# Attention scores of two heads on the two halves of TensorE's rows, in a two-layer decoder trunk

## The chip, the cores and the metric

The kernel runs on one core of a Trainium2 chip. The metric is the device time of one execution in microseconds (us), smaller is better. Three runs of the kernel before took 1722.72, 1716.74 and 1719.22 us: a median of 1719.22 us.

Engines are named as the profile names them: PE is TensorE's matmuls and PEld its weight loads, DVE is VectorE, ACT is ScalarE, POOL is GpSimd, SP is SyncE, whose queue issues the DMAs (its rows read SPq). "L381" is line 381 of the kernel.

## What is computed

Two layers over 1024 tokens of width 1024. The first mixes tokens with dilated sliding-window attention (three groups, 16 heads of 64), the second with grouped-query sliding-window attention (16 query heads over 2 key heads, with a learned sink logit per head). After each comes an output projection, a layer norm and a gated per-layer embedding. Cut to what matters here:

```python
def apply_rope(t, cos, sin):
    t1, t2 = t[..., :32], t[..., 32:]
    return concatenate([t1 * c - t2 * s, t2 * c + t1 * s], -1)

def banded_attention(q, k, v, max_dist, sinks=None):   # blocks of 128 queries
    s = einsum('bnqhgd,bnkhd->bnhgqk', qb, kw) * 64 ** -0.5
    s = where(mask, s, -inf)
    m = max(s, -1)                    # with sinks: m = maximum(m, sk)
    e = exp(s - m)
    l = sum(e, -1)                    # with sinks: l = l + exp(sk - m)
    return einsum('bnhgqk,bnkhd->bnqhgd', e, vw) / l, m + log(l)
```

## The kernel before

**Numbers.** Every factor of a product is split into two f16 parts, high and low, and three of the four products of parts are summed: high by high, high by low, low by high. A projection (`lin`, L262) so takes 24 matmuls of 128x512 for one tile of 128 tokens by 512 columns.

**Layer A** (`layer_a`, L620) goes twice over three groups. In each it takes a block of V weights and two blocks of Q and K weights; each block is multiplied with 8 tiles of tokens. **Layer B** (`layer_b`, L782) takes one block for keys and values, two for queries, two for the gate. Weight blocks come in by DMA, DVE takes their maximum (L108, four instructions a block), and ACT and DVE split them (L131, L132, four each), all in steps between the tiles.

**Rotation.** `rope_out` (L333) multiplies a projected tile in PSUM with cosine and sine on DVE (L344, twice), then POOL takes a difference for the first halves of the heads and a sum for the second (L346, L347). ACT rounds to the high part (L353) and POOL subtracts it (L354). One head's high and low parts, 64 columns each, lie side by side. For keys DVE copies them a second time with high and low exchanged (L357). One DMA transposes all blocks of 128 columns (L358): 4 queries, 4 keys and 4 exchanged keys in layer A. The transposed block of a head holds the high part on partitions 0 to 63 and the low one on 64 to 127, so a matmul over all 128 rows against the keys, and a second one against the exchanged keys, give the sum of all four products.

**Units.** The attention of 128 queries and four heads against one or two blocks of 128 keys is a unit; there are 96 in layer A and 32 in layer B. `scores` (L368) makes two PSUM tiles `s`, one for each pair of heads, fills each with its matmuls (L381), and has DVE add the mask and take the row maxima (L385, one instruction for each head and a short one that reads the maximum out). DVE then turns maxima into biases (L387; in layer B also L389, a minimum with the sinks), ACT takes the four exponentials (L391) and the f16 high part (L395), POOL or DVE the low part (L397), and a DMA transposes both to `pT` (L400). `pv` (L403) multiplies `pT` with the values, 12 matmuls of 64 columns for a block of keys (L412 to L414).

**Order.** `unit_step` (L298) takes up the scores of a new unit and the `pv` of the one taken up two units before (layer A) or three (layer B). Tiles come from pools of rotating buffers, and waits are put in where a buffer is written after a read. The program is then reordered for each engine by a list scheduler with a timeline of its own, so the order on an engine is not that of the code. Each engine runs its own instructions strictly in that order.

**Tables.** Cosines, sines, masks and the identity lie in one tile `tab`, loaded once at the start (L452, L458).

Of the kernel before, what the change touches and what calls it, by code (L numbers as in the profile page):

```python
# [20 lines left out]
P = 128  # L21
S = 1024
D = 1024
# [30 lines left out]
def const_table():  # L54
# [5 lines left out]
    for o in token_orders():  # L60
        for t in (cos, sin):
            rope.append(t[o].transpose(1, 0, 2).reshape(P, NT * 32))
# [22 lines left out]
N_ROPE = 6 * NT * 32  # L85
N_CONST = N_ROPE + 6 * P

# [51 lines left out]
class Trunk:  # L139
    def __init__(self, ctx, tc, a):  # L140
# [30 lines left out]
        self.cos, self.sin = [], []  # L171
        for o in range(3):
            for i, lst in enumerate((self.cos, self.sin)):
                b = (2 * o + i) * NT * 32
                lst.append(tab[:, b:b + NT * 32].rearrange("p (n c) -> p n c", n=NT))
        b = N_ROPE
# [13 lines left out]
    def keep(self, cols=1, name="k"):  # L190
        self.uid += 1
        return self.const.tile([P, cols], F32, name=f"{name}{self.uid}", tag=f"{name}{self.uid}")

# [139 lines left out]
    def rope_out(self, ps, nq, nk, order, n, dst):  # L333

        nc, w = self.nc, self.work
        nh = nq + nk
        t1 = w.tile([P, 512], F32, tag="t1", name="t1")
        t2 = w.tile([P, 512], F32, tag="t2", name="t2")  # L340
        pv = ps.rearrange("p (h c) -> p h c", c=32)
        for t, tb in ((t1, self.cos[order]), (t2, self.sin[order])):
            tv = t[:, :nh * HD].rearrange("p (h c) -> p h c", c=32)
            nc.vector.tensor_mul(tv, pv, tb[:, n, :].unsqueeze(1).to_broadcast([P, 2 * nh, 32]))  # L344
        v1, v2 = (t[:, :nh * HD].rearrange("p (h b c) -> p h b c", b=2, c=32) for t in (t1, t2))
        nc.gpsimd.tensor_sub(v1[:, :, 0, :], v1[:, :, 0, :], v2[:, :, 1, :])  # L346
        nc.gpsimd.tensor_add(v1[:, :, 1, :], v1[:, :, 1, :], v2[:, :, 0, :])  # L347
        nb = nh + nk
        hl = w.tile([P, 12, P], F16, tag="hl", name="hl", bufs=3)
        rv = t1[:, :nh * HD].rearrange("p (h c) -> p h c", c=HD)  # L350
# [17 lines left out]
    def scores(self, qa, kas, mask, cs, ncs, sums, nbias, floor, pool_lo):  # L368
# [65 lines left out]
    def startup(self):  # L434
# [4 lines left out]
        with tc.tile_pool(name="start", bufs=1) as st:  # L439
# [12 lines left out]
            nc.sync.dma_start(self.tab[:, N_CONST - P:], a["tab"][:, N_CONST - P:])  # L452
# [5 lines left out]
            nc.sync.dma_start(self.tab[:, :N_CONST - P], a["tab"][:, :N_CONST - P])  # L458
# [161 lines left out]
    def layer_a(self):  # L620
# [14 lines left out]
        for pair in range(2):  # L635
            for g in (1, 2, 0):
                blk = self.next_block()
# [9 lines left out]
                for i in range(2):  # L647
# [4 lines left out]
                    for n in range(NT):  # L652
                        ps = self.ps_lin.tile([P, 512], F32, tag="lin", name="lin")
                        self.lin(ps, blk, *self.stat_a(g, n), 0, 512)
                        qk.append(at.tile([P, 12, P], F16, tag="qk", name="qk", bufs=8))
                        self.rope_out(ps, 4, 4, g, n, qk[n])
# [22 lines left out]
    def unit_a(self, q, g, n, qk, vh, vl, cs, ncs, cv, scr):  # L679
# [22 lines left out]
        kas = [lambda h, sw, t=qk[i]: t[:, 4 + 4 * sw + h, :] for i in tiles]  # L702
        self.later(UNIT_LAG, lambda: self.unit(lambda h: qk[n][:, h, :], kas, mask, cs, ncs,
# [78 lines left out]
    def layer_b(self, xT, invx):  # L782
# [5 lines left out]
        self.nsink = self.kv.tile([P, 16], F32, name="nsink", tag="nsink")  # L788
        nc.vector.tensor_scalar(self.nsink, self.sinks, -1.0, LN_PSCALE, op0=ALU.mult, op1=ALU.add)
# [3 lines left out]
        kT = [self.kv.tile([P, 4, P], F16, tag=f"bk{n}", name="bk") for n in range(NT)]  # L793
        vh = self.kv.tile([P, NT, 2, HD], F16, tag="bvh", name="bvh")
        vl = self.kv.tile([P, NT, 2, HD], F16, tag="bvl", name="bvl")
        for n in range(NT):
# [3 lines left out]
            self.rope_out(ps[:, :P], 0, 2, 0, n, kT[n])  # L800
# [3 lines left out]
        for kv in range(2):  # L804
# [5 lines left out]
            nc.vector.tensor_scalar(ncs, cs, -1.0, None, op0=ALU.mult)  # L810
            for n in range(NT):
# [3 lines left out]
                self.rope_out(ps, 8, 0, 0, n, qT)  # L815
# [8 lines left out]
    def unit_b(self, kv, n, hg, qT, kT, vh, vl, cs, ncs, cv, tile_st):  # L824
        nc, at, sp = self.nc, self.att, self.small
        tiles = [n] if n == 0 else [n - 1, n]
        kas = [lambda h, sw, t=kT[i]: t[:, 2 * sw + kv, :] for i in tiles]
# [25 lines left out]
        self.later(UNIT_LAG, lambda: self.unit(lambda h: qT[:, 4 * hg + h, :], kas, mask, cs, ncs,  # L853
# [281 lines left out]
```

## Time and profile before

| | |
|---|---|
| median of 3 runs | 1719.22 us |
| the profiled execution, its own time | 1715.05 us |
| its span, first to last instruction | 1713.3 us |
| PE busy | 1595.0 us (93%) |
| DVE busy | 1163.1 us (68%) |
| ACT busy | 837.6 us (49%) |
| POOL busy | 700.2 us (41%) |
| mean granted clock of TensorE | 0.98 |

The busy time of PE counts a matmul from its start to its modelled end, and matmuls overlap; how much of PE a matmul really takes is read from the distance of one start to the next. Idle time before an instruction is put down to what ended it. The rows in question stand two sections below.

### The profile page before, as it was taken

The page shows a single profiled execution, that of the slowest core. Times are in us where ns is not written, and L with a number is a line of the kernel's source. Part 1 is how long each engine was busy: PE and PEld are TensorE (multiplying, and loading weights), DVE is VectorE, ACT ScalarE, POOL GpSimd, SP SyncE. Part 2 cuts the span into 40 slices and gives each one's busy share as a digit, 9 for nine tenths or more (in the row PEclk, how much of TensorE's full clock was granted, in tenths as well). Part 3 has the DMA queues.
Part 4 walks back from the last instruction along what each step waited for, and adds up shares of the span by engine and source line. Part 5 has one row for each costly group of instructions (what it writes and reads, how often), then busy time and mean ns, then how long its engine had stood idle before and what let it go on. Part 6 is the DMA issues. An engine that isn't in the chain of part 4 may idle for free. (4 is left out here: it accounts for less than half of the span.)

```text
span 1713.3 us, 29175 instructions
## 1 busy us (share of the span) xinstructions
PE 1595.0 (93%) x10579; PEld 882.3 (51%) x10579; DVE 1163.1 (68%) x2846; ACT 837.6 (49%) x1818; POOL 700.2 (41%) x601
## 2 busy tenths in 40 slices
PE   9899999999998889999999988689999898979998
PEld 3455566654555456666545543234464555534444
DVE  6767656765677776567567776787457988767731
ACT  4425554554654365545545663523334677753221
POOL 1115524532655665155235553443324553123431
PEclk9999999999999999999999999799999999989999
DMA  9618865764778787477558887989965798787963
GB/s 367 225 59 163 161 142 128 161 142 117 154 155 220 184 165 153 112 155 162 120 131 169 182 221 224 297 226 259 251 172 113 143 188 179 170 277 217 239 201 111
DMA packets 542785, 309.06 MB, mean 180 GB/s; under 512 B 473008, under 2 KB 494128, under 8 KB 542256
## 3 DMA queue, kind: packets, MB, share of 16 engines
q1 hardware_dynamic: 542640, 307.20, 73.2%
q8 instruction: 83, 1.36, 0.3%
q14 instruction: 62, 0.51, 0.1%
HBM read 135.82 MB, written 54.92 MB: 111 GB/s over the span
## 5 line engine op out<-in xcount | busy, mean ns | idle before, releaser
L268 PE MATMUL lin<-whl,xhl 128*128 128x512 f16 x1280 | 488.1, 381 | 0.0
L269 PE MATMUL lin<-whl,xhl 128*128 128x512 f16 x1280 | 486.9, 380 | 0.0
L270 PE MATMUL lin<-whl,xhl 128*128 128x512 f16 x1280 | 486.5, 380 | 0.0
L391 ACT ACTIVATE sm<-sm,st,cs 128x128 f32<-128x128 f32 (+1 forms) x384 | 203.6, 531 | 171.1 <-DVE st L387 144.2
L397 POOL TENSOR_TENSOR phl<-sm,phl 128x1024 f16<-128x1024 f32 (+1 forms) x88 | 160.3, 1821 | 257.2 <-ACT phl L395 240.5
L108 DVE TENSOR_REDUCE wpm<-wraw 128x1 f32<-128x1024 f32 (+1 forms) x132 | 156.8, 1197 | 93.2 <-DMA wraw<-in_wa_dram 49.8
L270 PEld LDWEIGHTS <-xhl 128*128 128x128 f16 x1280 | 149.0, 116 | 126.8 <-issue 1.9
L268 PEld LDWEIGHTS <-xhl 128*128 128x128 f16 x1280 | 149.0, 116 | 118.2 <-issue 1.8
L269 PEld LDWEIGHTS <-xhl 128*128 128x128 f16 x1280 | 149.8, 117 | 115.6 <-issue 1.3
L346 POOL TENSOR_TENSOR t<-t,t 128x256 f32<-128x256 f32 (+1 forms) x120 | 93.4, 778 | 275.1 <-DVE t L344 265.3
L354 POOL TENSOR_TENSOR hl<-t,hl 128x512 f16<-128x512 f32 (+1 forms) x120 | 140.2, 1169 | 102.5 <-ACT hl L353 102.5
L385 DVE CUSTOM_DVE_ANT_0 sm<-s,tab 128x256 f32<-128x256 f32 (+1 forms) x512 | 157.2, 358 | 30.8 <-PE s L381 26.5
L344 DVE TENSOR_TENSOR t<-lin,tab 128x512 f32<-128x512 f32 (+1 forms) x240 | 147.6, 654 | 28.0 <-PE lin L270 27.8
L132 DVE SCALAR_TENSOR_TENSOR whl<-wraw,s,whl 128x1024 f16<-128x1024 f32 (+1 forms) x116 | 156.6, 1394 | 3.1 <-ACT whl L131 3.1
L353 ACT ACTIVATE hl<-t 128x512 f16<-128x512 f32 (+1 forms) x120 | 72.3, 603 | 174.8 <-POOL t L347 155.7
L131 ACT ACTIVATE whl<-wraw,s 128x1024 f16<-128x1024 f32 (+1 forms) x116 | 122.0, 1123 | 21.7 <-DVE s L208 14.0
L268 PE MATMUL lin<-whl,x2T 128*128 128x512 f16 (+1 forms) x320 | 116.5, 364 | 0.0
L270 PE MATMUL lin<-whl,x2T 128*128 128x512 f16 (+1 forms) x320 | 116.2, 363 | 0.0
L269 PE MATMUL lin<-whl,x2T 128*128 128x512 f16 (+1 forms) x320 | 116.2, 363 | 0.0
L395 ACT ACTIVATE phl<-sm 128x1024 f16<-128x1024 f32 (+1 forms) x128 | 110.7, 865 | 2.2
L412 PEld LDWEIGHTS <-pT 128*128 128x128 f16 x800 | 72.4, 98 | 51.6 <-DMA pT<-phl 49.3
L357 DVE COPY hl<-hl 128x512 f16<-128x512 f16 (+1 forms) x104 | 50.4, 484 | 71.5 <-POOL hl L354 71.2
(189 smaller groups left out, 2940.1 us busy)
## 6 DMA issues: line engine op xcount, KB each, us to landing
wraw<-in_wa_dram SPq DMA_DIRECT2D x56, 512.0 KB, 5.5
scr<-st SPq DMA_DIRECT2D x96, 132.0 KB, 2.5
gt<-scr SPq DMA_DIRECT2D x48, 264.0 KB, 3.4
wraw<-in_wav_dram SPq DMA_DIRECT2D x24, 512.0 KB, 5.8
prh<-pro SPq DMA_DIRECT2D x32, 256.0 KB, 3.6
wraw<-in_wg_dram SPq DMA_DIRECT2D x16, 512.0 KB, 7.0
wraw<-in_wb_dram SPq DMA_DIRECT2D x16, 512.0 KB, 5.6
xg<-y SPq DMA_DIRECT2D x16, 512.0 KB, 3.8
```

Source lines behind the costliest of these rows:

```text
L108: k.nc.vector.tensor_reduce(pm[:, c:c + 1], self.raw[:, c * q:(c + 1) * q], axis=AX.X, op=ALU.max, apply_absolute_value=True)
L131: nc.scalar.activation(hl[:, 0, sl], self.raw[:, sl], AF.Copy, scale=self.s)
L132: nc.vector.scalar_tensor_tensor(hl[:, 1, sl], self.raw[:, sl], self.s, hl[:, 0, sl], op0=ALU.mult, op1=ALU.subtract)
L268: mm(ps, xh(kt), wh, start=(kt == 0), stop=False)
L269: mm(ps, xh(kt), wl, start=False, stop=False)
L270: mm(ps, xl(kt), wh, start=False, stop=(kt == NK - 1))
L344: nc.vector.tensor_mul(tv, pv, tb[:, n, :].unsqueeze(1).to_broadcast([P, 2 * nh, 32]))
L354: nc.gpsimd.tensor_sub(hl[:, :nh, HD:P], rv, hl[:, :nh, 0:HD])
L385: nc.vector.tensor_tensor_reduce(sm[:, h, :nk], ps[:, i, :nk], mask, 1.0, -3e38, ALU.add, ALU.max, mx[:, h:h + 1])
L391: nc.scalar.activation(sm[:, h, :nk], sm[:, h, :nk], AF.Exp, bias=nbias[:, h:h + 1], scale=cs, accum_out=sums[:, h:h + 1])
L395: nc.scalar.activation(hl[:, 0], sm[:, :, :nk], AF.Copy)
L397: eng.tensor_sub(hl[:, 1], sm[:, :, :nk], hl[:, 0])
```

## The change

**Scores.** High and low parts are no longer side by side for each head: all high parts come first, then all low parts. A transposed block of 128 columns then holds one part of two heads, head 0 of the pair on partitions 0 to 63 and head 1 on 64 to 127. A score matmul now reads 64 rows, the upper or the lower half (the program gives it a tile of 64x128 at row 0 or at row 64), and there are three for each head and block of keys: high by high, high by low, low by high. The copy of exchanged keys goes away, and the transposing DMAs have 8 blocks instead of 12 in layer A, 2 instead of 4 for the keys of layer B. The two PSUM tiles of a unit now belong to the two halves, and each holds the scores of that half's head for both pairs. In layer B the heads are reordered in the weights so that the two heads of a pair use different key heads.

**Biases.** DVE no longer computes the biases; one ACT instruction does. With sinks, DVE takes a maximum with scaled sinks ahead of it.

**Rotation.** The sine table holds minus sine and sine; DVE's second product reads the heads' halves exchanged, and POOL makes one sum of 512 columns instead of a difference and a sum of 256. The tables of a group are loaded when the group starts, 384 KB each, seven times in all, into two buffers.

```diff
-    def rope_out(self, ps, nq, nk, order, n, dst):
+    def rope_out(self, ps, nq, nk, n, dst):
...
-        for t, tb in ((t1, self.cos[order]), (t2, self.sin[order])):
-            tv = t[:, :nh * HD].rearrange("p (h c) -> p h c", c=32)
-            nc.vector.tensor_mul(tv, pv, tb[:, n, :].unsqueeze(1).to_broadcast([P, 2 * nh, 32]))
-        v1, v2 = (t[:, :nh * HD].rearrange("p (h b c) -> p h b c", b=2, c=32) for t in (t1, t2))
-        nc.gpsimd.tensor_sub(v1[:, :, 0, :], v1[:, :, 0, :], v2[:, :, 1, :])
-        nc.gpsimd.tensor_add(v1[:, :, 1, :], v1[:, :, 1, :], v2[:, :, 0, :])
+        cos = self.cos[:, n, :].unsqueeze(1).to_broadcast([P, 2 * nh, 32])
+        nc.vector.tensor_mul(t1[:, :nh * HD].rearrange("p (h c) -> p h c", c=32), pv, cos)
+        pb = ps.rearrange("p (h b c) -> p h b c", b=2, c=32)[:, :, ::-1, :]
+        sin = self.sin[:, n].unsqueeze(1).to_broadcast([P, nh, 2, 32])
+        nc.vector.tensor_mul(t2[:, :nh * HD].rearrange("p (h b c) -> p h b c", b=2, c=32), pb, sin)
+        nc.gpsimd.tensor_add(t1[:, :nh * HD], t1[:, :nh * HD], t2[:, :nh * HD])
...
-            nc.scalar.activation(hl[:, :nh, 0:HD], rv, AF.Copy)
-            nc.gpsimd.tensor_sub(hl[:, :nh, HD:P], rv, hl[:, :nh, 0:HD])
-            if nk:
-                src, to = (hl[:, a:b, :].rearrange("p h (w c) -> p h w c", w=2) for a, b in ((nq, nh), (nh, nb)))
-                nc.vector.tensor_copy(to, src[:, :, ::-1, :])
-            nc.sync.dma_start(dst, hl[:, :nb, :].rearrange("p b c -> p (b c)"), transpose=True)
+            nc.scalar.activation(hl[:, :m], t1[:, :m], AF.Copy)
+            nc.gpsimd.tensor_sub(hl[:, m:2 * m], t1[:, :m], hl[:, :m])
+            nc.sync.dma_start(dst, hl[:, :2 * m], transpose=True)
...
+        ps = [self.ps_s.tile([P, 2, 2 * P], F32, tag="s", name="s") for _ in range(2)]
         for pr in range(2):
-            ps = self.ps_s.tile([P, 2, 2 * P], F32, tag="s", name="s")
+            for kb, ka in enumerate(kas):
+                for j, (x, y) in enumerate(((0, 0), (0, 1), (1, 0))):
+                    for i in range(2):
+                        rows = slice(HD * i, HD * i + HD)
+                        nc.tensor.matmul(ps[i][:, pr, kb * P:(kb + 1) * P], qa(pr, x)[rows], ka(pr, y)[rows],
+                                         start=(j == 0), stop=(j == 2))
             for i in range(2):
                 h = 2 * pr + i
-                for kb, ka in enumerate(kas):
-                    for sw in range(2):
-                        nc.tensor.matmul(ps[:, i, kb * P:(kb + 1) * P], qa(h), ka(h, sw), start=(sw == 0),
-                                         stop=(sw == 1))
-            for i in range(2):
-                h = 2 * pr + i
-                nc.vector.tensor_tensor_reduce(sm[:, h, :nk], ps[:, i, :nk], mask, 1.0, -3e38, ALU.add, ALU.max,
+                nc.vector.tensor_tensor_reduce(sm[:, h, :nk], ps[i][:, pr, :nk], mask, 1.0, -3e38, ALU.add, ALU.max,
                                                mx[:, h:h + 1])
-        nc.vector.tensor_scalar(nbias, mx, ncs, LN_PSCALE, op0=ALU.mult, op1=ALU.add)
         if floor is not None:
-            nc.vector.tensor_tensor(nbias, nbias, floor, op=ALU.min)
+            nc.vector.tensor_max(mx, mx, floor)
+        nc.scalar.activation(nbias, mx, AF.Copy, scale=ncs, bias=LN_PSCALE)
```

**What the order becomes on PE.** The scheduler's order changes with it. In the kernel before, TensorE meets the second pair of a unit's heads right behind the first, in another PSUM tile. These rows are that place in a unit of layer A with two blocks of keys (`qk` holds transposed queries and keys; a DVE wait here is for a reader of an earlier unit):

```order
L381 LDWEIGHTS qk
L381 MATMUL s<-qk 128x128
L381 LDWEIGHTS qk [waits DVE_49]
L381 MATMUL s<-qk 128x128 [waits PE_49]
```

In the changed kernel the second pair goes into the same two PSUM tiles as the first, and its first matmul into each of them waits for DVE. These rows of PE are a second pair in layer A; its first pair stands 10 projection matmuls and 14 value matmuls ahead:

```order
L411 MATMUL o<-vl,pT 128x64
L379 LDWEIGHTS qk
L379 MATMUL s<-qk 128x128 [waits DVE_49]
L379 LDWEIGHTS qk
L379 MATMUL s<-qk 128x128
L379 LDWEIGHTS qk
L379 MATMUL s<-qk 128x128 [waits DVE_49]
...
L379 MATMUL s<-qk 128x128
L412 LDWEIGHTS pT
L412 MATMUL o<-vh,pT 128x64
```

The second pair has moved away from the first, here into the middle of another unit's value matmuls. Over the program the 1600 score matmuls of before stand in 149 uninterrupted stretches, the 2400 of the changed kernel in 259. Within these, 406 of the 2400 follow a matmul on the same half of the rows; taken in pairs of different halves where they alternate, they make 983 pairs and 434 single ones. In every unit the program's wait of the second pair names the reductions of the first; the projection and value matmuls in between are worth 1.2 to 7.6 us at the distances of [Rows 3] below, with a median of about 4.

**And on DVE.** Before, these rows of DVE are one unit of layer A (L385, four maxima), then its biases (L387), the copy of exchanged keys (L357) and the next tile's rotation (L344):

```order
L385 ISA sm,mx<-s,tab 128x256 [waits PE_49]
L385 ISA mx 128x1
L385 ISA sm,mx<-s,tab 128x256
L385 ISA mx 128x1
L385 ISA sm,mx<-s,tab 128x256 [waits PE_49]
L385 ISA mx 128x1
L385 ISA sm,mx<-s,tab 128x256
L385 ISA mx 128x1
L387 TENSOR_SCALAR st<-mx,ncs_4250 128x4 [waits DMAHW5_49,DVE_49]
L357 COPY hl<-hl 128x512 [waits DMAHW1_49,Pool_49]
L344 TENSOR_TENSOR t_4713<-lin,tab 128x512 [waits PE_49]
```

In the changed kernel the two pairs of a unit stand apart, here with a tile's rotation between them:

```order
L383 ISA sm,mx<-s,tab 128x256 [waits PE_49]
L383 ISA mx 128x1
L383 ISA sm,mx<-s,tab 128x256 [waits PE_49]
L383 ISA mx 128x1
L345 TENSOR_TENSOR t_4625<-lin,rope 128x512 [waits PE_49,Pool_49]
L348 TENSOR_TENSOR t_4626<-lin,rope 128x512
L383 ISA sm,mx<-s,tab 128x256 [waits DVE_49,PE_49]
L383 ISA mx 128x1
```

The biases and the copy are gone, and the rotation has moved between the first pair's maxima and the second's.

## Rows read from the trace of the kernel before

**Rows 1.** The page: span, then busy time, share and instructions of each engine.

```profile
span 1713.3 us, 29175 instructions
PE 1595.0 (93%) x10579; PEld 882.3 (51%) x10579; DVE 1163.1 (68%) x2846; ACT 837.6 (49%) x1818; POOL 700.2 (41%) x601
```

**Rows 2.** Windows of 100 us: busy us (instructions) of PE to POOL, PEclk, DMA share, GB/s.

```profile
500.00:600.00 100.00, 88.06 (x633) 50.37 (x632) 78.16 (x191) 45.79 (x109) 59.27 (x47) 0.95 0.77 192
700.00:800.00 100.00, 98.35 (x657) 67.88 (x656) 63.16 (x174) 51.92 (x133) 41.43 (x44) 1.00 0.66 138
1300.00:1400.00 100.00, 89.11 (x832) 51.72 (x830) 92.21 (x270) 64.91 (x172) 52.15 (x45) 0.97 0.76 153
```

**Rows 3.** Timeline of PE in layer A: start and length in us, instruction, count.

```profile
306.97 0.61 PE L381 MATMUL s<-qk 128*128 128x128 f16 x8
307.42 0.19 PE L412 MATMUL o<-vh,pT 128*128 128x64 f16 x1
307.45 0.19 PE L413 MATMUL o<-vl,pT 128*128 128x64 f16 x1
...
308.02 0.38 PE L269 MATMUL lin<-whl,xhl 128*128 128x512 f16 x1
...
314.71 0.38 PE L270 MATMUL lin<-whl,xhl 128*128 128x512 f16 x1
```

**Rows 4.** Groups by line and shape: busy us, mean ns of one, idle before.

```profile
L381 PE MATMUL s<-qk 128*128 128x128 f16 x1120 | 79.0, 220 | 5.4 <-DMA qk<-hl 5.3
L381 PEld LDWEIGHTS <-qk 128*128 128x128 f16 x1120 | 70.6, 98 | 26.8 <-DMA qk<-hl 7.2
L381 PE MATMUL s<-bk,bq 128*128 128x128 f16 x480 | 35.8, 221 | 2.1 <-DMA bq<-hl 2.1
```

**Rows 5.** Waits of PE alone: total us, times, longest us.

```profile
PE o L412 <- DMA pT<-phl: 39.8, 31, 4.0
PE s L381 <- DMA qk<-hl: 5.3, 2, 4.7
```

**Rows 6.** Waits of all engines, same columns.

```profile
DVE hl L357 <- POOL hl L354: 71.2, 42, 3.6
DVE sm L385 <- PE s L381: 26.5, 22, 2.8
```

**Rows 7.** Timeline of one unit of layer A, the last column what it waited for.

```profile
503.03 1.06 PE L381 MATMUL s<-qk 128*128 128x128 f16 x16
504.44 0.41 DVE L385 CUSTOM_DVE_ANT_0 sm<-s,tab 128x256 f32<-128x256 f32 x1
505.47 0.42 DVE L385 CUSTOM_DVE_ANT_0 sm<-s,tab 128x256 f32<-128x256 f32 x1
507.39 3.85 DVE L132 SCALAR_TENSOR_TENSOR whl<-wraw,s,whl 128x1024 f16<-128x1024 f32 x2
511.17 0.22 DVE L387 TENSOR_SCALAR st<-mx,ncs 128x4 f32<-128x4 f32 x1
511.42 0.60 ACT L391 ACTIVATE sm<-sm,st,cs 128x256 f32<-128x256 f32 x1 [2.57 <-DVE st L387]
```

**Rows 8.** Groups by line and shape on DVE, POOL and ACT, columns as in rows 4.

```profile
L385 DVE CUSTOM_DVE_ANT_0 sm<-s,tab 128x256 f32<-128x256 f32 x288 | 106.0, 416 | 19.3 <-PE s L381 15.0 <-POOL phl L397 4.3
L385 DVE DVE_READ_ACCUMULATOR2_ANT mx<- 128x1 f32 x512 | 41.3, 81 | 0.0
L387 DVE TENSOR_SCALAR st<-mx,ncs 128x4 f32<-128x4 f32 x96 | 40.9, 426 | 1.6
L387 DVE TENSOR_SCALAR sb<-mx,ncs 128x4 f32<-128x4 f32 x32 | 15.7, 493 | 0.3
L357 DVE COPY hl<-hl 128x512 f16<-128x512 f16 x96 | 48.6, 507 | 67.9 <-POOL hl L354 67.7
L132 DVE SCALAR_TENSOR_TENSOR whl<-wraw,s,whl 128x1024 f16<-128x1024 f32 x112 | 152.3, 1403 | 2.7 <-ACT whl L131 2.7
L346 POOL TENSOR_TENSOR t<-t,t 128x256 f32<-128x256 f32 x112 | 89.8, 802 | 266.6 <-DVE t L344 258.4 <-DVE se L842 3.3 <-DVE mde L224 3.0
L758 POOL TENSOR_TENSOR gt<-gt 128x512 f32<-128x512 f32 x16 | 22.7, 1419 | 1.0
L746 ACT ACTIVATE mw<-mw 128x24 f32<-128x24 f32 x16 | 3.5, 219 | 53.9 <-DVE mw L745 53.9
```

**Rows 9.** DMA issues: size or count, median us from issue to landing.

```profile
pT<-phl SPq DMA_TRANSPOSE x128, 4.4
qk<-hl SPq DMA_TRANSPOSE x96, 4.0
```

More of the change, by code (lines that the diff above doesn't have):

```diff
@@ L60, in const_table @@
     for o in token_orders():
-        for t in (cos, sin):
-            rope.append(t[o].transpose(1, 0, 2).reshape(P, NT * 32))
+        for t in (cos, np.concatenate([-sin, sin], 1)):
+            rope.append(t[o].transpose(1, 0, 2).reshape(P, -1))
     r = np.arange(P)[:, None]
@@ L170, in __init__ @@
         self.tab = tab
[L171 to L176, printed above, removed]
+        b = 0
         self.mask_a = tab[:, b:b + 2 * P]
@@ L192, in keep, with rope_tables @@
         return self.const.tile([P, cols], F32, name=f"{name}{self.uid}", tag=f"{name}{self.uid}")
+    def rope_tables(self, order):
+        t = self.const.tile([P, N_ROPE], F32, name="rope", tag="rope", bufs=2)
+        self.nc.sync.dma_start(t, self.a["tab"][:, order * N_ROPE:(order + 1) * N_ROPE])
+        self.cos = t[:, :NT * 32].rearrange("p (n c) -> p n c", n=NT)
+        self.sin = t[:, NT * 32:].rearrange("p (n b c) -> p n b c", n=NT, b=2)
     def pow2(self, mx, s, inv):
@@ L700, in outp @@
                 self.merges.append(self.merge(n, q // 2, scr[q // 2]))
-        kas = [lambda h, sw, t=qk[i]: t[:, 4 + 4 * sw + h, :] for i in tiles]
-        self.later(UNIT_LAG, lambda: self.unit(lambda h: qk[n][:, h, :], kas, mask, cs, ncs,
+        kas = [lambda j, x, t=qk[i]: t[:, 4 * x + 2 + j, :] for i in tiles]
+        self.later(UNIT_LAG, lambda: self.unit(lambda j, x: qk[n][:, 4 * x + j, :], kas, mask, cs, ncs,
                                           lambda h, kb: vh[:, tiles[kb], h, :], lambda h, kb: vl[:, tiles[kb], h, :],
@@ L787, in layer_b @@
         self.bufs = 3
-        self.nsink = self.kv.tile([P, 16], F32, name="nsink", tag="nsink")
-        nc.vector.tensor_scalar(self.nsink, self.sinks, -1.0, LN_PSCALE, op0=ALU.mult, op1=ALU.add)
+        self.rope_tables(0)
+        self.sk_cs = self.kv.tile([P, 16], F32, name="sk_cs", tag="sk_cs")
         blk = self.next_block()
@@ L792, in layer_b @@
         ck = self.prod(invx, blk.inv, 2.0 ** QK_SHIFT, "ck")
-        kT = [self.kv.tile([P, 4, P], F16, tag=f"bk{n}", name="bk") for n in range(NT)]
+        kT = [self.kv.tile([P, 2, P], F16, tag=f"bk{n}", name="bk") for n in range(NT)]
         vh = self.kv.tile([P, NT, 2, HD], F16, tag="bvh", name="bvh")
@@ L826, in unit_b @@
         tiles = [n] if n == 0 else [n - 1, n]
-        kas = [lambda h, sw, t=kT[i]: t[:, 2 * sw + kv, :] for i in tiles]
+        kas = [lambda j, x, t=kT[i]: t[:, x, :] for i in tiles]
         mask = self.mask_b[:, (2 - len(tiles)) * P:]
@@ L851, in outp @@
             nc.sync.dma_start(self.o_dr[n][:, c0 * HD:(c0 + 4) * HD], u)
-        self.later(UNIT_LAG, lambda: self.unit(lambda h: qT[:, 4 * hg + h, :], kas, mask, cs, ncs,
-                                          lambda h, kb: vh[:, tiles[kb], kv, :], lambda h, kb: vl[:, tiles[kb], kv, :],
-                                          stats, outp, hg == 1, self.nsink[:, c0:c0 + 4], after if hg else None))
+        self.later(UNIT_LAG, lambda: self.unit(lambda j, x: qT[:, 4 * x + 2 * hg + j, :], kas, mask, cs, ncs,
+                                          lambda h, kb: vh[:, tiles[kb], h % 2, :], lambda h, kb: vl[:, tiles[kb], h % 2, :],
+                                          stats, outp, hg == 1, self.sk_cs[:, c0:c0 + 4], after if hg else None))
     def transpose_rows(self, src, s, dst, i, name):
@@ L1106, in _layout, with heads @@
     a["ao"] = halves(f["a_w_out"][0])
-    a["bo"] = halves(f["b_w_out"][0])
+    turn = np.arange(16).reshape(2, 8).T.ravel()
+    def heads(m):
+        return m.reshape(m.shape[0], 16, HD)[:, turn].reshape(m.shape[0], 1024)
+    a["bo"] = halves(f["b_w_out"][0].reshape(16, HD, D)[turn].reshape(D, D))
     a["wg"] = np.stack([halves(f["ple_w_gate"][l]) for l in range(2)])
```

30 lines of the change are left out of this document (17 added, 13 removed).

## The prediction, made before the changed kernel ran

> **What bounds the kernel now.** I read the page's busy times first. PE is busy for 1595.0 of 1713.3 us, the next engine, DVE, for 1163.1 [rows 1]. Then the windows, because a mean hides stages: in 700 to 800 PE is busy for 98.35 us of 100, so there only PE's own work counts; in 500 to 600 it is 88.06 and in 1300 to 1400 89.11 with DVE at 92.21 [rows 2], so there something else sets the pace part of the time. What it is stands in the waits of PE: 39.8 us in 31 cases in front of a unit's first value matmul, for the transposed probabilities `pT` [rows 5]. There are 96 + 32 = 128 units (the counts of L387 in [rows 8]), so about 31 of 128 units, 24%, go at the pace of the chain from scores to `pT`, and the other 76% at the pace of PE.
>
> What one matmul takes of PE is the distance of starts. Eight score matmuls start at 306.97 and the next instruction at 307.42: 56 ns each. Two value matmuls are 29 ns apart (307.42, 307.45), projection matmuls 216 ns (31 steps from 308.02 to 314.71) [rows 3]. Each of them has a weight load of its own, and that load's record is 98 ns long [rows 4], so at these distances the loads run behind other matmuls.
>
> **The change part by part.**
>
> *Score matmuls.* Before: 1120 + 480 = 1600 [rows 4] by 56 ns = 89.6 us. After: 2400 of the same 128 columns. If two on different halves run at the same time, a pair takes the longer of one matmul (56 ns) and two issues with their loads (2 x 29 = 58 ns, the pace of the value matmuls). The order leaves 983 such pairs and 434 single ones: 983 x 58 + 434 x 56 ns = 81.3 us, **8.3 us less**. No row shows overlap. Bounds: all 1200 as pairs, 69.6 us (20 less); none overlapping, 2400 x 56 ns = 134.4 us (44.8 more). I take the overlap, since operands, rows and PSUM tiles of the two are separate.
>
> *Change of the tile's shape.* All matmuls of before use 128 rows, so no row shows TensorE going from 128 to 64 rows and back. The changed order does it 2 x 259 = 518 times. If it is free, 0. If the array has to be empty first, the matmul in front is waited for to its end: 0.38 - 0.216 us for a projection (its record's length less the step, [rows 3]) and 220 - 56 ns for a score [rows 3, 4], both 165 ns: 518 x 165 ns = 85 us. If the first load can't hide either, 98 ns more each: 136 us. I take half of the 165 ns, 82 ns, since a recorded end is modelled and holds more than the way through the array: **42.7 us**. [...]
>
> *A new wait inside each unit.* The second pair's matmuls now wait for the first pair's maxima on DVE. What is queued behind them on PE is everything: value and projection matmuls. DVE needs two maxima of 416 + 81 ns [rows 8], 1.0 us, once it gets to them, and it seldom does at once: it was found idle and waiting for scores only 22 times [rows 6] in 256 pairs. In the unit of [rows 7] the maxima start 1.4 us after the scores, and a run of weight splits that follows holds DVE for 3.85 us. The order covers the wait with 1.2 to 7.6 us of other matmuls, about 4 at the median. A run of four splits is 4 x 1.403 = 5.6 us [rows 8], 1.6 beyond the cover; some 24 blocks are split in the attention stages, 24 x 1.6 = 38 us if each run met a waiting pair. I take a third, **12 us**. Bounds: 0, and 38.
>
> *The chain to `pT`.* The second pair's scores come about 4 us later than before. Shorter by: two maxima, since the first pair's are done by then, 1.0 us; the biases' step on DVE, 0.43 us (L387), taken over by ACT at about 0.22 (L746) with the same four exponentials behind it; the copy L357, 0.51 us, and DVE's wait for POOL ahead of it, 71.2 us over 104 copies, 0.68 each [rows 6, 8]. 4.0 - 1.0 - 0.43 + 0.22 - 0.51 - 0.68 = 1.6 us longer. A unit's values come two units after its scores, so in the 31 units that wait, each costs half of it, 0.8 us: 25 us. In [rows 7] the biases stood behind 5.4 us of other DVE work after the last maximum began, which the change takes out of the chain there, so I take **18**. Bounds: 0, and 31 x 1.5 = 46 (the 3 us without any relief).
>
> *Relief of DVE in layer B.* L387 leaves: 15.7 us [rows 8]. In 1300 to 1400 DVE and PE are about equally close to full [rows 2], so half counts: **8 us less**. Bounds: 0 and 15.7. Layer A's share (40.9 + 48.6 us) is hidden under PE, other than in the chain above.
>
> *No cost:* POOL's one sum, at most 1419 (L758) instead of twice 802 ns (L346) [rows 8], with POOL 41% busy. The transposes of `qk` with a third fewer blocks: they land in 4.0 us [rows 9], and PE waited for them 5.3 us in all [rows 5]; that is what it would give at most. Seven loads of tables on SP's queue: each is issued as its group starts and first read a V block later, 8 x 24 x 216 ns = 41 us of cover; without that cover one would cost some 4 us.
>
> *Sum.* PE's own work: -8.3 + 42.7 + 12 = 46.4 us, of which 76% reach the end: 35. With 18 and -8: +45. The profiled execution took 1715.05 us, so 1760; the median of the runs is 4.2 us above it, so **1764 us**.
>
> **Rivals.**
>
> *Faster: TensorE changes shape for nothing.* Then 518 x 82 ns go, and if DVE, with 40.9 + 15.7 + 48.6 us less to do and 71.2 us less to wait, keeps ahead of the second pairs, so do the 12. -8.3 x 0.76 = -6; half of the chain's 18, +9; relief 15.7: together -13, **1706 us**. For it: at 56, 29 and 216 ns TensorE passes from one kind of matmul to another without a gap [rows 3]. Against it: these all have the same shape. It decides below 33 ns a change: with the other terms as here, (-8.3 + 518 x 0.033) x 0.76 + 9 - 15.7 = 0.
>
> *Slower: the change of shape costs the whole way out.* 165 ns: (-8.3 + 85 + 12) x 0.76 + 10 = +77, **1797 us**; with the load in the open, 1835. For it: the two differences in the rows agree at 165 ns. [...]
>
> *The change doesn't do what it says: halves run one after another.* Then +44.8 in place of -8.3: (44.8 + 42.7 + 12) x 0.76 + 10 = +86, **1805 us**; with a free change of shape +53, 1772. For it: a matmul of 64 rows has as many columns as one of 128, and no row shows two at once. [...]
>
> **How the numbers follow.** Forecast (1764): 0.44. Free change of shape (1706): 0.26. Full price (1797 to 1835): 0.17. No overlap (1772 to 1805): 0.13. The range has to leave out no more than 0.2: from 1700, below the faster case with its chain bound at 0, to 1820, past no overlap and the nearer half of the full price. Within 0.3% is 1714 to 1724 us, about what a measurement of this kernel can tell from no change. The faster case lies under it 3 times in 4 (0.195), the forecast's own low end now and then (0.015): faster 0.21. Same 0.07, from the upper end of the faster case and the lower end of the forecast. Slower 0.72.
>
> **What would show it.** In the profile of the changed kernel: starts of score matmuls in twos a few ns apart, pairs some 58 ns apart, show the overlap; 56 ns throughout refute it. The distance from the last projection matmul to the first score matmul, and from the last score to the next projection matmul, beyond 216 and 56 ns, is the price of a change of shape: about 80 ns each by the forecast, nothing or 165 by the rivals. Waits of PE's scores on L383, near 12 us or more, show the new wait; hardly any refute it. Waits for `pT` above 39.8 us show the longer chain, below it that the relief weighs more. The forecast is wrong if the changes of shape are free and PE's waits fall: then the time is under 1714.

## The result, and the profile after

The changed kernel takes **1739.6 us** (median of 4 runs, 1738.5 to 1745.6) against 1719.3 us: ratio 1.0124, 95% interval 1.0094 to 1.0154. The profiled execution took 1738.61 us with a span of 1736.8, 23.5 more than before. So it is slower by 1.2%, in the direction and inside the range of the forecast, but by 20 us in place of 45. All times here are medians of executions in one state of the chip; one execution of e2_halves (1922.4 us at a granted clock of 0.84) belongs to a slower state and is left out.

The page of the changed kernel, span and engines, as [rows 1]:

```profile
span 1736.8 us, 30492 instructions
PE 1637.7 (94%) x11379; PEld 859.0 (49%) x11379; DVE 1105.9 (64%) x2617; ACT 870.8 (50%) x1946; POOL 679.9 (39%) x481
```

DVE is 57 us less busy and PE 43 us more. The timeline of PE in layer A of the changed kernel, columns as in [rows 3]:

```profile
155.99 0.38 PE L271 MATMUL lin<-whl,xhl 128*128 128x512 f16 x1
156.21 0.38 PE L272 MATMUL lin<-whl,xhl 128*128 128x512 f16 x1
156.52 0.34 PE L379 MATMUL s<-qk 64*128 64x128 f16 x6
156.79 0.41 PE L270 MATMUL lin<-whl,xhl 128*128 128x512 f16 x1
...
194.46 0.34 PE L379 MATMUL s<-qk 64*128 64x128 f16 x6
194.73 0.20 PE L410 MATMUL o<-vh,pT 128*128 128x64 f16 x1
194.77 0.19 PE L411 MATMUL o<-vl,pT 128*128 128x64 f16 x1
```

Two things stand here. First, the six score matmuls of one pair of heads fit between 156.52 and 156.79: by their single records the starts lie 3, 64, 2, 54 and 2 ns apart, so the two halves run at the same time. Second, the step from the last projection to the first score is 0.31 us, where one projection follows another after 0.22; and from the last score's start to the next projection 148 ns pass, where 56 ns was a score's step before. Over the program the medians are 312 in place of 216 ns, 148 in place of 56, and 126 in place of 29 (value to score): **92 to 97 ns for each change of the tile's shape**, in either direction.

Waits of PE in the changed kernel, columns as in [rows 5]:

```profile
PE o L410 <- DMA pT<-phl: 29.9, 21, 3.6
...
PE s L379 <- DVE mx L383: 10.6, 11, 1.6
PE s L379 <- DMA qk<-hl: 3.2, 3, 1.4
```

A second wait of value matmuls, in layer B, before and in the changed kernel (`mu` is written where VectorE scales the output of an earlier unit, whose PSUM tile `o` the matmuls write again):

```profile
PE o L412 <- DVE mu L849: 14.2, 8, 3.9
PE o L410 <- DVE mu L852: 1.1, 1, 1.1
```

And one wait of DVE in the changed kernel:

```profile
DVE sm L383 <- PE s L379: 105.7, 74, 3.3
```

The new wait of a second pair for the first pair's maxima is there, 10.6 us. But the waits of the value matmuls for `pT` fell from 39.8 to 29.9 us [rows 5], where the forecast had them rise, and those for `mu`, which neither [rows 5] nor the forecast lists, fell by 13.1. And DVE now stands idle ahead of the scores 74 times for 105.7 us, before 22 times for 26.5 [rows 6]: it is ahead of TensorE where it used to be level with it.

**An account of TensorE** in the two attention stages, from the first score matmul to the last value matmul of each layer. It is worked out from the distances between the starts of PE's instructions: from each distance the instruction's own step is taken (216, 109, 56 or 29 ns by its columns; between two scores in halves up to 60 ns), from one between a score and something else up to 96 ns for the change of shape, and what is left is a wait, put to the kind of matmul that came late. Sums are of unrounded values.

| us, layers A + B | before | changed |
|---|---|---|
| score matmuls, own | 62.5 + 26.8 = 89.3 | 52.8 + 25.4 = 78.2 |
| changes of shape (none; 389 + 127) | 0 | 36.6 + 12.0 = 48.6 |
| waits in front of scores | 6.4 + 0.5 = 6.8 | 17.7 + 2.6 = 20.3 |
| waits in front of value matmuls | 45.1 + 20.3 = 65.4 | 30.8 + 6.7 = 37.5 |
| waits in front of projections and others | 5.5 + 4.6 = 10.1 | 9.5 + 4.5 = 14.0 |
| projections, own (count) | 861.4 (3991) | 876.1 (4059) |

The account takes every step as it is at a granted clock of 1.0. In 23.9 us of these two stages before, and in 26.4 in the changed kernel, the granted clock was 0.5, the lower clock below; there a projection's step was 427 ns in place of 216 and a value matmul's 53 in place of 29 (medians of both kernels). What the slower steps take more, by these numbers some 10 us in both, stands in the rows of waits, most of it in the last. In other runs this part is 6 to 23 us, and it is named below where a reading hangs on it.

TensorE's own work on scores and shapes is up by 48.6 - 11.1 = 37.5 us, all its waits are down by 82.4 - 71.8 = 10.6. The 68 projection matmuls more (14.7 us) are not new work: the order has brought them forward from later stages. Layer A's stage is 37.5 us longer and layer B's 4.2; between the two 11.4 us less pass and behind layer B 6.8 less, which makes the +23.5.

So the question for the experiments: the price on TensorE came as forecast. Why did the waits fall, where the forecast had +12 in front of scores, +18 in front of values and -8 in layer B?

### The profile page after: what moved, and what is told of

The parts are those of the page before. It is cut to its first block, busy times and chain, and to the rows that moved or that the text cites. A ratio compares the mean times of both kernels' runs of the same rounds, so it can differ in the third digit from the quotient of the medians.

```text
span 1736.8 us, 30492 instructions
## 1 busy us (share of the span) xinstructions
PE 1637.7 (94%) x11379; PEld 859.0 (49%) x11379; DVE 1105.9 (64%) x2617; ACT 870.8 (50%) x1946; POOL 679.9 (39%) x481
## 5 line engine op out<-in xcount | busy, mean ns | idle before, releaser
L349 POOL TENSOR_TENSOR t<-t,t 128x512 f32<-128x512 f32 (+1 forms) x120 | 152.4, 1270 | 262.8 <-DVE t L348 235.0
L383 DVE CUSTOM_DVE_ANT_0 sm<-s,tab 128x256 f32<-128x256 f32 (+1 forms) x512 | 165.6, 359 | 111.9 <-PE s L379 105.7
L355 POOL TENSOR_TENSOR hl<-t,hl 128x512 f16<-128x512 f32 (+1 forms) x120 | 147.5, 1230 | 119.6 <-ACT hl L354 119.5
L132 DVE SCALAR_TENSOR_TENSOR whl<-wraw,s,whl 128x1024 f16<-128x1024 f32 (+1 forms) x116 | 181.9, 1614 | 6.6 <-ACT whl L131 6.5
L345 DVE TENSOR_TENSOR t<-lin,rope 128x512 f32<-128x512 f32 (+1 forms) x120 | 79.2, 660 | 110.7 <-PE lin L272 91.1
L387 ACT ACTIVATE st<-mx,ncs 128x4 f32<-128x4 f32 x96 | 28.2, 293 | 159.3 <-DVE mx L383 159.1
L379 PE MATMUL s<-qk 64*128 64x128 f16 x1680 | 87.0, 219 | 13.4 <-DVE mx L383 9.2
```

What stands on the lines that cost most here:

```text
L132: nc.vector.scalar_tensor_tensor(hl[:, 1, sl], self.raw[:, sl], self.s, hl[:, 0, sl], op0=ALU.mult, op1=ALU.subtract)
L349: nc.gpsimd.tensor_add(t1[:, :nh * HD], t1[:, :nh * HD], t2[:, :nh * HD])
L355: nc.gpsimd.tensor_sub(hl[:, m:2 * m], t1[:, :m], hl[:, :m])
L383: nc.vector.tensor_tensor_reduce(sm[:, h, :nk], ps[i][:, pr, :nk], mask, 1.0, -3e38, ALU.add, ALU.max, mx[:, h:h + 1])
```

## The experiments

Two theories for the fall of the waits. **Relief**: with the biases on ScalarE and less on VectorE, `pT` is ready sooner. **Slack**: TensorE itself became slower, so `pT` is there when it comes. They differ in what each part of the change does alone. All times are medians with the ratio to the kernel before on the same chip.

**e1_relief: the kernel before with the two small edits (and the tables loaded by group, which belongs to the second) and without the halves.**

```diff
-        nc.vector.tensor_scalar(nbias, mx, ncs, LN_PSCALE, op0=ALU.mult, op1=ALU.add)
...
+        nc.scalar.activation(nbias, mx, AF.Copy, scale=ncs, bias=LN_PSCALE)
...
+        nc.gpsimd.tensor_add(t1[:, :nh * HD], t1[:, :nh * HD], t2[:, :nh * HD])
...
```

Expected: 

> The kernel before with the change's other parts alone: biases on ScalarE and one rotary sum with the tables loaded by group; scores stay as they were, 1600 matmuls over all rows, and the copy of swapped keys stays. Theory 'relief' (the waits for pT fell in the changed kernel, by 28 us in front of value matmuls, because the chain from scores to pT got shorter): those waits fall from 65 to some 40 to 45 us here too and the time is near 1700 us. Theory 'slack' (they fell because TensorE itself got slower, so that pT is there when it is asked for): they stay within some 10 us of before and the time is 1712 to 1722 us.

Measured: 1695.3 us, ratio 0.9863 (0.9832 to 0.9893), faster than both kernels. Its waits of PE:

```profile
PE o L414 <- DMA pT<-phl: 29.4, 22, 3.2
```

That is the same 29 us as in the changed kernel, on full rows and with TensorE as quick as before. By the account the waits in front of value matmuls are 46.5 us, 18.9 less than before, and the time is close to what relief said. Relief.

**e2_halves: the changed kernel with both small edits undone.**

```diff
+        nc.vector.tensor_scalar(nbias, mx, ncs, LN_PSCALE, op0=ALU.mult, op1=ALU.add)
...
-        nc.scalar.activation(nbias, mx, AF.Copy, scale=ncs, bias=LN_PSCALE)
...
-        nc.gpsimd.tensor_add(t1[:, :nh * HD], t1[:, :nh * HD], t2[:, :nh * HD])
...
+        nc.gpsimd.tensor_sub(v1[:, :, 0, :], v1[:, :, 0, :], v2[:, :, 1, :])
+        nc.gpsimd.tensor_add(v1[:, :, 1, :], v1[:, :, 1, :], v2[:, :, 0, :])
```

Expected: 

> The changed kernel with the biases back on VectorE and the rotary sum back as a difference and a sum on GpSimd: the halves alone, without the copy of swapped keys. Changes of the tile's shape still cost about 94 ns each, near 500 of them. Theory 'relief': the waits for pT are back at 60 us or more and the time is 1755 to 1765 us. Theory 'slack': they stay near the 37 us of the changed kernel and the time is within 8 us of its 1739.5 us.

Measured: 1772.6 us, ratio 1.0318 (1.0283 to 1.0352), above both ranges and nearer to that of relief. Two of its waits of PE:

```profile
PE o L410 <- DMA pT<-phl: 39.5, 22, 5.5
PE s L379 <- DVE mx L383: 14.0, 12, 3.0
```

The halves alone cost 52 us, and without the small edits the wait for `pT` is back at 39.5. The account puts waits in front of scores at 27.8 and in front of values at 50.3. The sum of the two is 78.1, before it was 72.3: the second pairs' wait is 21 us more, and 15 less are waited for later, in front of the values. The layers differ in this. In layer A 14.8 more in front of scores stand against 3.3 less in front of values; in layer B 6.1 against 11.7, and what went there is the wait for `mu`, 1.1 us here as in the changed kernel. In this kernel all waits together are 97.5 us, with both edits 71.8, which is the relief again (some 7 of these 25.7 us are steps at the lower clock). DVE's idle time ahead of the scores is 99.9 us here and 31.3 in e1_relief: DVE ahead of TensorE belongs to the halves, not to the relief.

**e4_padded: the kernel before with seven idle matmuls more in each of the 128 units**, 896 x 56 ns = 50.2 us of work for TensorE.

```diff
+            for _ in range(4 - pr):
+                nc.tensor.matmul(ps[:, 0, :P], self.ones, self.ones, start=True, stop=True)
```

Expected: 

> The kernel before with seven idle matmuls of 128x128 ahead of each unit's scores (four and three ahead of the two pairs), 56 ns each: 128 x 7 x 56 ns = 50 us of TensorE's time and nothing else; their results are overwritten. Theory 'slack': the waits for pT fall by 20 to 30 us and the time rises by only 20 to 30 us, to 1740 to 1750. Theory 'relief': the waits fall by 10 us at most and the time rises by 40 us or more, to 1759 and up.

Measured: 1774.7 us, ratio 1.0327 (1.0293 to 1.0361), 54 us more. Its waits of PE:

```profile
PE o L414 <- DMA pT<-phl: 47.1, 22, 5.2
```

Hardly any of the 50 us is swallowed by waits: in front of the value matmuls they are 62.1 us, before 65.4. Steps at the lower clock take some 7 us more than before. The slack theory falls, and with it the 76% of the forecast.

**e3_scores_first: the changed kernel with both pairs' matmuls ahead of the first maximum**, which removes the second pairs' wait and half of the changes of shape (132 stretches of scores in place of 259, and 8 matmuls in place of 406 behind one on the same half).

```diff
                         nc.tensor.matmul(ps[i][:, pr, kb * P:(kb + 1) * P], qa(pr, x)[rows], ka(pr, y)[rows],
                                          start=(j == 0), stop=(j == 2))
+        for pr in range(2):
             for i in range(2):
```

Expected: 

> The changed kernel with the score matmuls of both pairs written ahead of the first maximum, so that no score matmul waits for the same unit's maxima: 132 stretches of score matmuls instead of 259. If each change of shape costs 94 ns whatever surrounds it, 254 fewer give 24 us back; nearly perfect pairs (1200 instead of 1417 steps) give another 10, the missing wait 10. Theory 'slack': a quarter to a half of these 44 us comes back as waits for pT: 1706 to 1718 us, about level with the kernel before. Theory 'relief': nearly all of it stays gained: 1695 to 1704 us, faster than both kernels.

Measured: 1735.3 us, ratio 1.0091 (1.0062 to 1.0121), a miss for both. Its waits of PE:

```profile
PE o L411 <- DMA pT<-phl: 55.7, 25, 4.9
```

On TensorE it does what it should: scores 68.7 us, changes 24.7, waits in front of scores 8.0. But the waits in front of values rise to 71.7, 34 us above the changed kernel. Ten of the units of layer A whose `pT` came late have transposes of 7 to 11.5 us from issue to landing, where the median is 4.2; e1_relief has four such units. Two more runs ask whether that is lateness alone.

**e7_first_lag3 and e10_first_lags: the same with more lead**, in layer A a unit's values three units after its scores, and in the second run in layer B four in place of three as well.

```diff
-        self.set_lag(2)
+        self.set_lag(3)
...
-        self.set_lag(3)
+        self.set_lag(4)
```

Expected of the first: 

> The halves with both pairs' matmuls ahead of the first maximum (1735.3 us, 71.7 us of waits in front of the value matmuls), and in layer A a unit's values three units after its scores in place of two. Theory lateness: those waits are pT coming late (transposes of 7 to 11 us in the late units), and the earlier scores leave too little between scores and values: with one unit more the 48.8 us of layer A fall under 15, and the time to 1695 to 1710. Theory elsewhere: the waits only show that another engine or the DMA queue sets the pace, so they come back in front of scores or projections and the time stays 1725 to 1740.

Expected of the second: 

> Halves with both pairs' matmuls ahead of the first maximum and three units of lead in layer A (1702.9 us), and in layer B four units in place of three. Waits in front of the value matmuls are 20.9 us in layer B. Lateness: they fall under 8, and the time to 1688 to 1693. Elsewhere: 1698 to 1705, with the waits in front of scores or projections instead.

Measured: 1702.9 us, ratio 0.9906 (0.9874 to 0.9937), and 1693.6 us, ratio 0.9849 (0.9813 to 0.9886). Waits of PE of the first:

```profile
PE o L411 <- ACT st L689: 18.7, 7, 5.0
PE lin L270 <- DMA ogT<-rhl: 17.6, 5, 11.8
PE o L411 <- DMA pT<-phl: 16.5, 9, 4.3
```

The 48.8 us in front of layer A's values are 21.8 now, none of it for `pT`: the first line is a wait for ScalarE, which reads an earlier unit's `o`, and the 16.5 us of the third lie in layer B. So for this order it was lateness. Of the 32 us that come off the time, layer A's stage has 25 in the profiles (922.8 to 897.7 us); the rest lies between the two layers. In layer B, against the expectation, the unit more takes only 1 us off the waits in front of values: those for `pT` fall from 16.5 to 6.3, but 11.9 for `mu` come in their place. That stage is 10 us shorter, some 7 of them since less of it ran at the lower clock (6.8 us against 20.5), and by their intervals the two runs just can't be told apart. With enough lead, halves cost little: by the account 68.7 + 24.7 = 93.4 us of scores and changes, against 89.3 on full rows.

**e8_halves_lag3: the changed kernel with three units of lead in layer A.**

```diff
-        self.set_lag(2)
+        self.set_lag(3)
```

Expected: 

> The changed kernel, with a unit's values three units after its scores in layer A in place of two. Its waits in front of the value matmuls are 30.8 us in layer A, and its changes of shape cost some 49 us over both layers. Theory: what the halves lose is TensorE's own time (changes of shape) and the wait inside the units, neither of which more lead takes away, so only the waits for pT fall, by 15 to 20 us: 1718 to 1727 us. Rival: the wait inside the units (11.4 us more in layer A) goes too, since other matmuls can stand between: 1705 to 1715.

Measured: 1744.8 us, ratio 1.0147 (1.0115 to 1.0179): not faster than the changed kernel, so both theories miss. Its waits of PE:

```profile
PE s L235 <- DVE mdd L228: 32.0, 2, 27.1
PE o L410 <- DMA pT<-phl: 17.0, 11, 6.2
PE s L379 <- DVE mx L383: 15.7, 9, 3.6
```

The wait for `pT` is 13 us less, the second pairs' wait for the maxima 5 us more. By the account layer A has 10 us less in front of values and 3.9 + 4.5 more in front of scores and projections, and all waits of the attention stages stay at 71 us: part of what is taken away at one place is waited for at another, and the 4.5 are steps at the lower clock (29.7 us of layer A's stage ran at it, in the changed kernel 16.1). The longest wait of the first line, 27.1 us, is the end of layer A, where a chain over all units is waited for; the changed kernel has 22.8 there.

**e5_bias and e6_rotary: e1_relief split in two.** The first has only the biases on ScalarE, the second only the one rotary sum; both load the tables by group, as e1_relief does; no run has these loads alone.

Expected of the first: 

> The kernel before with the biases of the exponentials on ScalarE and the rotary tables by group, the rotary difference and sum as two operations on GpSimd as before. It splits the 25 us that both reliefs together brought on full rows (1695.3 us). The forecast's own chain has 0.43 - 0.22 = 0.2 us for the biases against 0.51 + 0.68 = 1.2 us for the rotary, 15% and 85%: by that this kernel gains 4 us, 1716. Rival: the biases stand in the middle of the chain, behind whatever VectorE has queued after the last maximum, 5.4 us in the unit shown ahead of the prediction, so they bring most, 18 us: 1702. Waits in front of the value matmuls, 65.4 us before and 46.5 with both: about 62 by the first, about 51 by the second.

Expected of the second: 

> The kernel before with one rotary sum on GpSimd and the tables by group, the biases on VectorE as before. By the forecast's own chain this brings 85% of the 25 us: 1699, waits in front of the value matmuls about 49 us. By the rival (the biases bring most) 7 us: 1713, waits about 60. If the two effects do not simply add, this and the run with the biases alone miss 25 us together by more than 8.

Measured: **1688.3 us**, ratio 0.982 (0.9782 to 0.9857), and 1718.5 us, ratio 0.9998 (0.9978 to 1.0017). All of the gain comes with the biases, and the forecast's split of the chain, 15% and 85%, was upside down. The groups on ACT tell how. These are the exponentials of layer A in the kernel before (busy us, mean ns of one, idle before):

```profile
L391 ACT ACTIVATE sm<-sm,st,cs 128x128 f32<-128x128 f32 (+1 forms) x384 | 203.6, 531 | 171.1 <-DVE st L387 144.2 <-issue 22.5 <-DVE m L214 4.5
```

With the biases on ScalarE (e5_bias):

```profile
L393 ACT ACTIVATE sm<-sm,st,cs 128x128 f32<-128x128 f32 (+1 forms) x384 | 203.6, 532 | 3.4
L391 ACT ACTIVATE st<-mx,ncs 128x4 f32<-128x4 f32 x96 | 28.1, 293 | 111.9 <-DVE mx L387 111.7
```

With the rotary sum alone (e6_rotary):

```profile
L393 ACT ACTIVATE sm<-sm,st,cs 128x128 f32<-128x128 f32 (+1 forms) x384 | 203.5, 531 | 169.9 <-DVE st L389 137.2 <-issue 22.7 <-DVE m L216 6.2
```

Before, ScalarE stood idle for 171 us ahead of these exponentials, 144 of them for the biases on VectorE; with its own biases it is idle 112 us for the maxima and works 28. From the last score to `pT` landed a unit took on average 13.3, 17.5 and 21.1 us before (52 units of layer A with one block of keys, 44 with two, 28 of layer B with two), with the biases on ScalarE 12.3, 16.1 and 19.7, with the rotary sum 13.2, 17.4 and 21.3. That is 1.0 to 1.4 us for the biases, where their own durations differ by 0.1 to 0.2 (426 and 493 ns in [rows 8] against 293 and 291), and nothing for the rotary sum. About half of it lies between the end of the last maximum and the first exponential (1.4, 1.6 and 3.2 us before, 0.9, 0.8 and 2.4 with the biases on ScalarE), the other half ahead of the last maximum, which VectorE gets to sooner. The two attention stages are 19.4 us shorter in e5_bias; the rest of its 29 us lies mostly between the layers. e5_bias and e1_relief, both edits, can't be told apart by their intervals.

**e11_halves_bias: the changed kernel with the rotary sum as two operations again.**

```diff
-        nc.gpsimd.tensor_add(t1[:, :nh * HD], t1[:, :nh * HD], t2[:, :nh * HD])
...
+        nc.gpsimd.tensor_sub(v1[:, :, 0, :], v1[:, :, 0, :], v2[:, :, 1, :])
+        nc.gpsimd.tensor_add(v1[:, :, 1, :], v1[:, :, 1, :], v2[:, :, 0, :])
```

Expected: 

> The changed kernel with the rotary difference and sum as two operations on GpSimd again, so the halves with the biases on ScalarE alone. On full rows the biases brought 30 us and the rotary sum nothing. If that holds on the halves too: 1735 to 1745, as the changed kernel. If the rotary sum matters there (less on GpSimd ahead of VectorE's copies and maxima): 1755 to 1765.

Measured: 1754.7 us, ratio 1.0202 (1.0167 to 1.0238), 18 us below e2_halves and 15 above the changed kernel, just short of the second range. The 15 do not lie in the attention stages: all waits there are 75.2 us, in the changed kernel 71.8. They lie behind layer A, where 384 matmuls of the output projections need 82.9 us: that stage takes 84.5 us in the changed kernel and 102.8 here. Waits of PE in that stretch (1117 to 1221 us) of e11_halves_bias; its first line is the end of layer A, which the changed kernel has too:

```profile
PE lin L270 <- issue: 19.5, 1, 19.5
PE lin L270 <- DVE rs L210: 6.1, 1, 6.1
PE lin L270 <- DMA ogT<-rhl: 3.3, 1, 3.3
PE lin L270 <- DVE p2t L201: 2.4, 1, 2.4
```

There TensorE waits for the next tile of attention outputs: its scales (L201, L210) come late on VectorE, and with them its split and transposed copy `ogT`. As each of the last three waits ended, the granted clock was 0.5 for 6.8, 3.4 and 3.4 us; over the stretch it is 0.92, in the changed kernel 0.98, and estimated from these stretches, that is some 6 of the 18 us. The same stage has 11.6 us more than its matmuls before, 17.6 in e3_scores_first, 19.9 here, and 1.6 in the changed kernel, but also 1.7 in e2_halves, which has the same two operations as this run. What decides it from kernel to kernel was not settled; so whether the rotary sum is worth anything on the halves stays open.

**e9_relief_lag3 and e12_bias_lag4: more lead for the full rows**, in e1_relief three units in layer A (with six `qk` tiles in place of eight to make room), in e5_bias four units in layer B.

Expected of the first: 

> Full rows with both reliefs (1695.3 us, 46.5 us of waits in front of the value matmuls, 35.1 of them in layer A), three units between scores and values in layer A, and six qk tiles in place of eight to make room. Theory lateness: the 35.1 us fall under 12, and the time to 1670 to 1680. Theory elsewhere, or qk tiles that come free too late: 1690 to 1700.

Expected of the second: 

> Full rows with the biases on ScalarE (1688.3 us) and four units of lead in layer B in place of three; its waits in front of the value matmuls are 15.6 us there. Lateness: under 6, 1677 to 1682. Elsewhere: 1685 to 1691.

Measured: 1703.8 us, ratio 0.9913 (0.988 to 0.9945), and 1688.4 us, ratio 0.9823 (0.9791 to 0.9855). Neither gains. The first:

```profile
PE s L235 <- DVE mdd L228: 37.2, 2, 32.2
PE o L414 <- ACT st L692: 16.4, 8, 4.4
...
PE s L383 <- DMA qk<-hl: 11.6, 6, 2.3
PE o L414 <- DMA pT<-phl: 8.5, 6, 2.8
```

Layer A's waits in front of values fall by 14.6 us, as the lateness theory had it, but 7.4 come back in front of scores (`qk` tiles are fewer), 5 in front of projections, and the wait at the end of layer A is 10 us longer. Why is not shown: with three units of lead too, e7_first_lag3 and e8_halves_lag3 take 48.9 and 52.7 us from layer A's last value matmul to its first output projection, where the same kernels with two units take 55.0 and 52.4. In e12_bias_lag4 the 15.6 us in front of layer B's values did not move at all (15.7): most of them are not lateness of `pT`, which is waited for 4.0 us there in e5_bias, against 9.4 for `mu`.

All waits of the attention stages side by side (us): before 82.4, rotary sum alone 86.0, biases alone 63.2, both 63.0; halves alone 97.5, with the biases 75.2, with both 71.8. Biases take 19 to 22 us of waits away wherever they are moved; the halves add 9 to 15; and no order with more lead came below 59. Without the steps at the lower clock the seven are some 72, 69, 57 and 52, then 80, 68 and 61: 12 to 15 us for the biases, 8 to 11 for the halves.

## Why the prediction was right and wrong

**Halves at the same time: right.** 983 pairs and 434 single ones gave -8.3 us; measured -11.1. The rival in which they run one after another falls.

**Change of the tile's shape: right, and the half was a lucky choice.** Forecast 82 ns x 518 = 42.7 us; measured 92 to 97 ns, 48.6 us for the 516 changes in the two stages. Free change (1706) and full price (1797 to 1835) fall. The bound of 165 ns came from records' lengths; how much of a record is the way through the array, from which the half was taken, was the author's estimate and no run shows it. By the distances of starts the step grows by 96 ns from a projection to a score, by 97 from a value matmul to a score and by 92 from a score to either; what TensorE does in that time was not shown.

**The wait inside the unit: its place and size right.** Forecast 12 us; in front of scores 13.5 us more were measured, 21 more with the halves alone. In e2_halves, layer B, the waits in front of values fall by more than those in front of scores rise (11.7 against 6.1), in layer A by far less (3.3 against 14.8).

**The chain to `pT`, +18: this is the step that failed.** Measured in front of the value matmuls: -27.9 us, 14.3 of them in layer A and 13.6 in layer B. In layer A the second pair that comes later, 4.0 us a unit in the forecast, did not lengthen these waits (-3.3 with the halves alone, where TensorE waits ahead of the scores instead), and the two edits took 11.0 off. Its list of reliefs had the right entries with wrong sizes. The biases stood in it with the difference of two durations, 0.43 - 0.22 us; e5_bias shows 1.0 to 1.4 us a unit and 19.4 us off the two stages, because the instruction waits its turn in VectorE's queue behind whatever is there. The unit of [rows 7] showed just that: 5.7 us from the last maximum's start to the biases (the forecast reads 5.4), and the forecast used it only to choose 18 rather than 25. The copy of exchanged keys and the wait ahead of it (71.2 us in [rows 6]) stood with 1.2 us; the rotary sum that was to shorten that wait gives nothing on full rows (e6_rotary), and no run took the copy away alone. In layer B the forecast had the wrong wait: before, 14.2 of the 20.3 us in front of values were for `mu` on VectorE and 3.2 for `pT`, and the 14.2 are 1.1 with the halves alone as in the changed kernel. In e4_padded they are 2.3, with 13.3 for `pT` in the layer: more work on TensorE alone takes them away too, but whether that is what the halves do stays open.

**Relief of VectorE: -8 in layer B, and nothing in layer A "under PE": the same failure from its other side.** e5_bias has 14.1 us off layer A's stage, which was to get nothing, and 5.3 off layer B's.

**Of TensorE's work 76% reach the end: wrong.** e4_padded: 50.2 us of work gave 54 us. Here a busy share was no share of what passes through. With 100% the forecast's own terms would have made 46.4 + 18 - 8 = 56 us and 1776 in place of 1764; this error hid part of the other.

**No cost: held as far as it could be seen.** POOL's one sum costs nothing on full rows (e6_rotary, ratio 0.9998), and PE's waits for `qk` fell from 5.3 to 3.2 us.

In sum: TensorE's own 34.4 us were forecast and 37.5 came; the waits were to bring 22 and brought -10.6, of which the halves alone make +15.1 and the two edits -25.7. The sign came out right since the first is larger than the second, and the prediction's own condition for its error, waits for `pT` below 39.8 us, is what the profile after shows. The best of the runs leaves the halves out: the kernel before with its biases on ScalarE alone, 1688.3 us, 1.8% under the kernel before and 2.9% under the changed one. With the halves, e10_first_lags comes within 5 us of it (1693.6), and their intervals overlap: what the halves cost hangs on the order of the scores and on the lead.

## What to carry to other kernels

Two edits that come together should be priced, and if possible run, apart: here one part of the change gained 25 to 33 us and the other lost 44 to 52. An instruction that stands in a chain between two engines can cost what its queue makes it wait, not its own duration (the biases: 1.0 to 1.4 us a unit, where the durations differ by 0.1 to 0.2); the row to read is the idle time of the engine that comes after it (here 144 us of ScalarE's). And in this kernel, with TensorE 93% busy, each microsecond of work added to it was about a microsecond of the time (e4_padded: 50.2 us of work, 54 us of time), while the 33 us of work that e3_scores_first took away from the changed kernel brought 4, until the units had more lead.

## What the runs showed of the hardware

- A pair of matmuls of 64 rows on the two halves starts mostly 2 to 4 ns apart (median 3) and the next pair 56 ns after it at the median, the step of one matmul of 128 rows, so in the changed kernel two took the time of one.
- Each change between tiles of 128 and of 64 rows lengthened PE's step by 92 to 97 ns, with projections and with value matmuls on the other side (312 ns in place of 216, 126 in place of 29, 148 in place of 56). Estimated from these steps, a stretch of scores pays some 190 ns in all: with 6 matmuls, three pairs, that is more than the 168 ns of their own, and full rows need 224 ns for the same scores; with 24, as in many units of e3_scores_first, it is 190 beside 670, and full rows need 896.
